# Two 16x16 row substitutions of a gated DeltaNet, put into one set of steps on VectorE

## The chip, the cores and the metric

The kernel runs on one core of one Trainium2 chip. The metric is the device time of one execution in microseconds (us). Engines are TensorE (PE in the rows; its weight loads are PEld), VectorE (DVE), ScalarE (ACT), GpSimd (POOL) and SyncE (SP, which issues the DMAs). Each engine works through its own list of instructions in a fixed order, and semaphores make one engine wait for another.

## What is computed

A backbone of two layers over 256 context tokens and 256 latent tokens. Each layer is a token mixer (three head groups side by side: S5, gated DeltaNet (GDN), Mamba-2) and a feed-forward net (dense in layer 0, eight experts in layer 1). The part at hand is the triangular solve of GDN, once for each direction of the sequence:

```python
kb = k * beta[..., None]
lower = jnp.where(strict, jnp.einsum("bhnid,bhnjd->bhnij", kb, k) * decay, 0.0)
sol = lax.linalg.triangular_solve(jnp.eye(CHUNK, dtype=F32) + lower, rhs,
                                  left_side=True, lower=True, unit_diagonal=True)
```

The second direction is the same on the reversed sequence, so its matrices are triangular the other way.

## The kernel before

The kernel solves by building inverses of the triangular matrices: first those of all 16x16 diagonal blocks, by row substitution, then blocks of 32, 64 and 128 by matrix products. `gdn_prep` makes the 16x16 inverses. The 512 tokens lie as 4 tiles (t) of 128 partitions, with 4 heads (h): a partition is a row of a block, and along the free dimension stand the 16 (t, h) pairs times the 16 columns. So one VectorE instruction works on all 128 blocks (8 along the partitions, 16 along the free dimension) of one direction at once.

For each layer it gathers the diagonal blocks into `c16` (lines 855 to 863), makes for each direction `u` (the block times beta, masked to its triangle, lines 872 and 874) and `x` (set to the identity, line 875), and then takes 15 steps. In each step, for each of the two directions: a stream shuffle on VectorE broadcasts row kk of each block over its 16 partitions (`row`, line 885), a multiply on GpSimd makes `prod` (line 886), and a subtract on VectorE updates the columns of `x` that can be nonzero (line 887). Step number k has n = k+1 columns, so its instructions have 16n elements a partition: 16 to 240. Direction 0 goes down from row 15 with columns kk to 15, direction 1 goes up from row 0 with columns 0 to kk. The two directions don't depend on one another.

What reads the result: `inverses` in `gdn` multiplies `x` into block-diagonal tiles `iv_X` on GpSimd (line 919), and then the products of the levels follow, with `iv_Q` (line 935) and `iv_X` (line 938) on VectorE. The temporary tiles of `gdn_prep` are in a pool that is closed behind it; the pool of `m2_decays` (tiles `dq_r`, `dq_W`, `dq_E`, lines 771, 776, 1065 to 1067) comes to lie on the same memory, so its first tiles wait for the last reader there.

What stands beside it on VectorE: `wL` (line 324), the low half of each weight tile split in two for TensorE (its high half `wH`, line 323, is ScalarE's); the taps of the convolutions `cv_acc` (line 795); in layer 0 the tables of S5 (`cm_a` to `cm_d` and `WV`, lines 430 to 435); the S5 scan (`s5B`, line 607, with its products `s5t` on GpSimd, line 604).

The order on each engine is not written out by hand. A planner fixes it when the program is built: it simulates the engines and picks from what is ready by priority, and the priority is a "band", a number where the smaller goes first. The substitution stands in band 2.0 in layer 0 and 12.62 in layer 1 (`pb`); `wL` in 1.8 and 12.4 (`w`); the qkv convolutions in 2.0 and 12.0, those of Mamba-2 in 3.0 and 13.0 (`xb`); the S5 tables in 1.5 and 2.5; the S5 scan in 3.5 and 12.5; `inverses` in 2.0 to 2.12 and 12.0 to 12.1.

Of the kernel before, what the change touches and what calls it, by code (L numbers as in the profile page):

```python
# [10 lines left out]
F32 = mybir.dt.float32  # L11
# [3 lines left out]
OP = mybir.AluOpType  # L15
# [75 lines left out]
class Net:  # L91
# [741 lines left out]
    def gdn_prep(self, p, tp, kT, qT, bs, sm, t0):  # L833

        nc = self.nc
        sh = [128, 4, 128]
        kw, qw = [], {}
        c32 = tp.tile([128, 4, 4, 32], F32, name="gd_c32")

        def product(f, W, name):  # L840
            ps = self.ps()
            for h in range(4):
                self.mm(ps[:, h * 128:(h + 1) * 128], kT[:, h, sl], f(h), start=True, stop=True, skip_group_check=True)
            m = p.tile(sh, F32, name=name)
            nc.vector.tensor_tensor(m, ps.rearrange("p (h c) -> p h c", h=4), W, op=OP.mult)
            return m

        for t in range(4):
            sl = slice(t * 128, (t + 1) * 128)
            W = tp.tile(sh, F32, name="gd_W")  # L850
            self.decay_quad(tp, sm, t, 16, W, "px", 1)
            kw.append(product(lambda h: kT[:, h, sl], W, f"gd_kw{t}"))
            for q in range(4):
                r = slice(q * 32, q * 32 + 32)
                nc.scalar.activation(c32[r, t], kw[t][r, :, r], AF.Copy)
            if t * 128 >= t0:
                so = slice(t * 128 - t0, (t + 1) * 128 - t0)
                qw[t] = product(lambda h: qT[:, h, so], W, f"gd_qw{t}")
        s16 = [128, 16, 16]
        c16 = tp.tile(s16, F32, name="gd_c16", tag="gd_prod0")  # L860
        cv = c32.rearrange("p t h c -> p (t h) c")
        nc.vector.tensor_scalar(c16, cv[:, :, 0:16], self.half16[:, 0:1], None, op0=OP.mult)
        nc.vector.scalar_tensor_tensor(c16, cv[:, :, 16:32], self.half16[:, 1:2], c16, op0=OP.mult, op1=OP.add)

        def bc(m):
            return m.unsqueeze(1).to_broadcast(s16)

        U, X = [], []
        for d in range(2):
            u = tp.tile(s16, F32, name=f"gd_u{d}")  # L870
            x = p.tile(s16, F32, name=f"gd_x{d}")
            nc.vector.tensor_tensor(u.rearrange("p (t h) c -> p t h c", t=4), c16.rearrange("p (t h) c -> p t h c", t=4),
                                    bs[:, :, d, :].unsqueeze(3).to_broadcast([128, 4, 4, 16]), op=OP.mult)
            nc.vector.tensor_tensor(u, u, bc(self.up16 if d == 0 else self.lo16), op=OP.mult)
            nc.vector.tensor_copy(x, bc(self.id16))
            U.append(u)
            X.append(x)
        for k in range(15):
            for d in range(2):
                kk = 15 - k if d == 0 else k  # L880
                cs = slice(kk, 16) if d == 0 else slice(0, kk + 1)
                n = cs.stop - cs.start
                row = tp.tile(s16, F32, name=f"gd_row{d}")[:, :, :n]
                prod = tp.tile(s16, F32, name=f"gd_prod{d}", tag=f"gd_prod{d}")[:, :, :n]
                nc.vector.stream_shuffle(row, X[d][:, :, cs], [16 * (i // 16) + kk for i in range(32)])
                nc.gpsimd.tensor_tensor(prod, row, U[d][:, :, kk:kk + 1].to_broadcast([128, 16, n]), op=OP.mult)
                nc.vector.tensor_tensor(X[d][:, :, cs], X[d][:, :, cs], prod, op=OP.subtract)
        return kw, qw, X

    def gdn(self, l, p, kT, qT, vD, kD, prep, nrm, bs, ks, qss, sm, szD, yD, t0, b0):  # L890
# [1097 lines left out]
```

## Time and profile before

| | |
|---|---|
| median of 3 runs | 2574.26 us (2572.71 to 2578.19) |
| the profiled execution | 2575.22 us, its span 2573.4 us |
| PE busy | 2384.3 us (93%) |
| DVE busy | 1866.9 us (73%) |
| ACT busy | 1441.4 us (56%) |
| POOL busy | 373.0 us (14%) |

A busy time is summed over the whole span. The page cuts the span into 40 slices of 64 us; the substitution of layer 0 lies in slices 4 and 5 (counted from 1: the fourth and fifth), that of layer 1 in slices 22 and 23. A timeline row gives start, duration, engine, line, operation, tiles, shape and count, and in brackets the idle time of the engine before it with what ended it.

### The profile page before, as it was taken

How to read it: one execution, taken by the hardware profiler on the slowest of the kernel's cores; microseconds unless marked ns; L12 is line 12 of the kernel's file. 1: busy time of each engine (PE TensorE's matmuls, PEld its weight loads, DVE VectorE, ACT ScalarE, POOL GpSimd, SP SyncE). 2: the span in 40 equal slices, each digit the busy share in tenths (PEclk: the TensorE clock that was granted, in tenths of full speed). 3: DMA queues.
4: the chain of work that ended last, by engine and by line, in shares of the span. 5: the costliest groups of instructions: out<-in, count | busy, mean ns of one | idle time of the engine just before them, and what ended most of it. 6: DMA issues, size and time to landing. Idle time of an engine off the chain costs nothing. (4 is left out here: it accounts for less than half of the span.)

```text
span 2573.4 us, 36183 instructions
## 1 busy us (share of the span) xinstructions
PE 2384.3 (93%) x12758; PEld 1864.3 (72%) x12758; DVE 1866.9 (73%) x3011; ACT 1441.4 (56%) x2223; POOL 373.0 (14%) x435
## 2 busy tenths in 40 slices
PE   7999876899999999998988799999999999999997
PEld 4778755556666888886876666587888888888876
DVE  8686998446548765445688954468888888888886
ACT  4676556433234554335766622347777777777765
POOL 0001677312000000000074621100000000000000
PEclk9899988999999999999998899999999999999999
DMA  7343322786635445323543466577999999999993
GB/s 245 114 124 116 119 94 72 238 245 215 233 106 166 146 132 175 103 86 106 163 139 121 152 200 181 171 259 291 346 340 339 356 342 338 353 345 341 353 344 148
DMA packets 222763, 543.87 MB, mean 211 GB/s; under 512 B 26992, under 2 KB 90480, under 8 KB 189552
## 3 DMA queue, kind: packets, MB, share of 16 engines
q1 hardware_dynamic: 222576, 541.50, 61.7%
q8 instruction: 102, 1.67, 0.3%
q14 instruction: 85, 0.70, 0.1%
HBM read 487.87 MB, written 53.54 MB: 210 GB/s over the span
## 5 line engine op out<-in xcount | busy, mean ns | idle before, releaser
L1664 DVE TENSOR_TENSOR mwL<-mwr,mwH 128x2048 fp32r<-128x2048 f32 (+1 forms) x272 | 605.0, 2226 | 95.3 <-PE bank L162 59.8
L1663 ACT ACTIVATE mwH<-mwr 128x2048 fp32r<-128x2048 f32 (+1 forms) x272 | 508.2, 1869 | 202.5 <-PE bank L162 166.4
L323 ACT ACTIVATE wH<-wr 128x512 fp32r<-128x512 f32 (+2 forms) x388 | 232.9, 605 | 400.5 <-PE bank L162 293.7
L324 DVE TENSOR_TENSOR wL<-wr,wH 128x512 fp32r<-128x512 f32 (+2 forms) x388 | 280.9, 726 | 220.2 <-ACT wH L323 199.3
L162 PE MATMUL bank<-mwL,xeH 128*128 128x512 f32 (+1 forms) x768 | 292.7, 381 | 9.3 <-DVE mwL L1664 9.3
L162 PE MATMUL bank<-mwH,xeL 128*128 128x512 f32 (+1 forms) x768 | 288.0, 375 | 0.0
L162 PE MATMUL bank<-mwH,xeH 128*128 128x512 f32 (+1 forms) x768 | 284.6, 376 | 1.7 <-ACT mwH L1663 1.7
L162 PE MATMUL bank<-hH,wH 128*128 128x512 f32 (+2 forms) x656 | 247.5, 385 | 21.8 <-ACT hH L301 8.1
L162 PE MATMUL bank<-hH,wL 128*128 128x512 f32 (+2 forms) x656 | 250.7, 383 | 16.0 <-DVE wL L324 15.9
L162 PE MATMUL bank<-hL,wH 128*128 128x512 f32 (+2 forms) x656 | 248.9, 380 | 1.1 <-DVE hL L302 1.1
L162 PE MATMUL bank<-ada,sc 128*32 128x512 f32 (+1 forms) x576 | 149.7, 503 | 27.0 <-DMA ada<-in_ada_first_dram 13.3
L795 DVE SCALAR_TENSOR_TENSOR cv_acc<-cv_raw,pp,cv_acc 128x512 f32<-128x512 f32 (+1 forms) x192 | 162.8, 861 | 12.1 <-issue 6.1
L162 PEld LDWEIGHTS bank<-mwL,xeH 128*128 128x128 f32 x768 | 144.3, 188 | 37.7 <-DVE mwL L1664 11.7
L162 PEld LDWEIGHTS bank<-mwH,xeH 128*128 128x128 f32 x768 | 144.1, 188 | 31.4 <-ACT mwH L1663 2.5
L162 PEld LDWEIGHTS bank<-mwH,xeL 128*128 128x128 f32 x768 | 144.3, 188 | 26.3
L162 PEld LDWEIGHTS bank<-hH,wH 128*128 128x128 f32 (+1 forms) x656 | 126.5, 194 | 49.6 <-ACT hH L301 10.6
L162 PEld LDWEIGHTS bank<-hH,wL 128*128 128x128 f32 (+1 forms) x656 | 126.7, 193 | 43.9 <-DVE wL L324 20.7
L162 PEld LDWEIGHTS bank<-hL,wH 128*128 128x128 f32 (+1 forms) x656 | 126.8, 193 | 25.8 <-DVE hL L302 2.2
L162 PE MATMUL bank<-mwL,eaH 128*128 128x512 f32 x352 | 139.2, 395 | 0.0
L162 PE MATMUL bank<-fhH,wH 128*128 128x512 f32 x352 | 136.8, 392 | 2.3 <-ACT fhH L301 1.4
L162 PE MATMUL bank<-fhL,wH 128*128 128x512 f32 x352 | 138.8, 394 | 0.0
L162 PE MATMUL bank<-mwH,eaL 128*128 128x512 f32 x352 | 138.6, 394 | 0.0
(440 smaller groups left out, 4715.0 us busy)
## 6 DMA issues: line engine op xcount, KB each, us to landing
mwr<-in_moe_gu_dram SPq DMA_DIRECT2D x176, 1024.0 KB, 5.9
mwr<-in_moe_dn_dram SPq DMA_DIRECT2D x80, 1024.0 KB, 6.1
wr<-in_w_in_dram SPq DMA_DIRECT2D x160, 256.0 KB, 3.0
ada<-in_ada_w_dram SPq DMA_DIRECT2D x128, 256.0 KB, 3.4
wr<-in_w_out_dram SPq DMA_DIRECT2D x64, 256.0 KB, 3.1
wr<-in_ffn_w_gate_dram SPq DMA_DIRECT2D x44, 256.0 KB, 2.7
wr<-in_ffn_w_up_dram SPq DMA_DIRECT2D x44, 256.0 KB, 2.8
ada<-in_ada_first_dram SPq DMA_DIRECT2D x32, 256.0 KB, 5.3
```

The source lines that it names most:

```text
L162: return self.nc.tensor.matmul(*a, **k)
L323: nc.scalar.activation(wH, w, AF.Copy)
L324: nc.vector.tensor_tensor(wL, w, wH.bitcast(F32), op=OP.subtract)
L795: nc.vector.scalar_tensor_tensor(acc, raw[:, :, j:j + 256], w[:, j:j + 1], acc, op0=OP.mult, op1=OP.add)
L1663: nc.scalar.activation(wH, w, AF.Copy)
L1664: nc.vector.tensor_tensor(wL, w, wH.bitcast(F32), op=OP.subtract)
```

## The change

Both directions are put into one tile `X` and one tile `U`, with the direction as an extra dimension. Direction 1 is mirrored: a stream shuffle with a mirrored list of partitions, written through an access pattern of step -1, turns its lower triangle into an upper one, so that both directions take the same steps with the same row and the same columns. A step is then three instructions on VectorE, each with 32n elements: shuffle, multiply (in place in `row`), subtract. GpSimd has no part in it. In the end direction 1 is mirrored back into `x1` and direction 0 copied into `x0`. The temporary tiles need 8 KB a partition where they needed 6 KB. Nothing else is edited.

```diff
-        c16 = tp.tile(s16, F32, name="gd_c16", tag="gd_prod0")
+        c16 = tp.tile(s16, F32, name="gd_c16")
...
-        U, X = [], []
-        for d in range(2):
-            u = tp.tile(s16, F32, name=f"gd_u{d}")
-            x = p.tile(s16, F32, name=f"gd_x{d}")
+        mirror = [16 * (i // 16) + 15 - i % 16 for i in range(32)]
+        U = tp.tile([128, 2, 16, 16], F32, name="gd_u")
+        X = tp.tile([128, 2, 16, 16], F32, name="gd_x")
+        u1 = tp.tile(s16, F32, name="gd_u1")
+        for d in (1, 0):
+            u = u1 if d else U[:, 0]
...
-            nc.vector.tensor_tensor(u, u, bc(self.up16 if d == 0 else self.lo16), op=OP.mult)
-            nc.vector.tensor_copy(x, bc(self.id16))
-            U.append(u)
-            X.append(x)
-        for k in range(15):
-            for d in range(2):
-                kk = 15 - k if d == 0 else k
-                cs = slice(kk, 16) if d == 0 else slice(0, kk + 1)
-                n = cs.stop - cs.start
-                row = tp.tile(s16, F32, name=f"gd_row{d}")[:, :, :n]
-                prod = tp.tile(s16, F32, name=f"gd_prod{d}", tag=f"gd_prod{d}")[:, :, :n]
-                nc.vector.stream_shuffle(row, X[d][:, :, cs], [16 * (i // 16) + kk for i in range(32)])
-                nc.gpsimd.tensor_tensor(prod, row, U[d][:, :, kk:kk + 1].to_broadcast([128, 16, n]), op=OP.mult)
-                nc.vector.tensor_tensor(X[d][:, :, cs], X[d][:, :, cs], prod, op=OP.subtract)
+            nc.vector.tensor_tensor(u, u, bc(self.lo16 if d else self.up16), op=OP.mult)
+        nc.vector.stream_shuffle(U[:, 1, :, ::-1], u1, mirror)
+        nc.vector.tensor_copy(X, self.id16.unsqueeze(1).unsqueeze(1).to_broadcast([128, 2, 16, 16]))
+        for k in range(15, 0, -1):
+            n = 16 - k
+            row = tp.tile([128, 2, 16, 16], F32, name="gd_row")[:, :, :, :n]
+            nc.vector.stream_shuffle(row, X[:, :, :, k:], [16 * (i // 16) + k for i in range(32)])
+            nc.vector.tensor_tensor(row, row, U[:, :, :, k:k + 1].to_broadcast([128, 2, 16, n]), op=OP.mult)
+            nc.vector.tensor_tensor(X[:, :, :, k:], X[:, :, :, k:], row, op=OP.subtract)
+        x1 = p.tile(s16, F32, name="gd_x1")
+        x0 = p.tile(s16, F32, name="gd_x0")
+        nc.vector.stream_shuffle(x1, X[:, 1, :, ::-1], mirror)
+        nc.vector.tensor_copy(x0, X[:, 0])
+        X = [x0, x1]
```

## Rows read from the trace of the kernel before

**Rows 1.** The page: busy tenths of each engine in 40 slices of 64 us.
```profile
PE   7999876899999999998988799999999999999997
DVE  8686998446548765445688954468888888888886
POOL 0001677312000000000074621100000000000000
```

**Rows 2.** Stretches: us, busy time (instructions) per engine, granted clock, DMA share, GB/s.
```profile
253.00:280.00 27.00, 27.00 (x129) 22.38 (x127) 23.97 (x95) 16.37 (x24) 13.22 (x23) 1.00 0.54 157
280.00:450.00 170.00, 120.48 (x658) 97.97 (x656) 160.66 (x204) 97.19 (x199) 122.27 (x116) 0.88 0.26 85
...
1380.00:1400.00 20.00, 12.12 (x37) 8.58 (x35) 11.86 (x45) 19.75 (x29) 6.77 (x16) 0.83 0.44 158
...
1400.00:1480.00 80.00, 67.06 (x339) 52.72 (x340) 79.42 (x137) 52.28 (x119) 49.58 (x58) 0.89 0.49 155
1480.00:1640.00 160.00, 158.56 (x1023) 104.05 (x1021) 76.51 (x151) 46.44 (x121) 28.87 (x26) 1.00 0.64 189
```

**Rows 3.** Waits from 250 to 480 us: total, times, longest.
```profile
PE bank L162 <- DVE iv_Q L935: 22.3, 7, 7.3
```

**Rows 4.** Groups of instructions by line: count, busy us, mean ns, idle before.
```profile
L886 POOL TENSOR_TENSOR gd_prod<-gd_row,gd_u 128x16 f32<-128x16 f32 (+14 forms) x60 | 38.1, 645 | 57.5 <-DVE gd_row L885 40.4 <-DVE gd_u L874 16.1
...
L887 DVE TENSOR_TENSOR gd_x<-gd_x,gd_prod 128x16 f32<-128x16 f32 (+14 forms) x60 | 20.8, 362 | 2.5 <-POOL gd_prod L886 1.9
L885 DVE STREAM_SHUFFLE gd_row<-gd_x 128x16 f32<-128x16 f32 (+14 forms) x60 | 18.0, 328 | 0.0
```

**Rows 5.** Timeline of VectorE in layer 0: substitution, S5 tables, `wL`, convolution.
```profile
253.58 0.42 DVE L430 TENSOR_TENSOR cm_a<-WV,mr 128x256 f32<-128x256 f32 x1
253.91 0.42 DVE L431 TENSOR_TENSOR cm_c<-WV,mi 128x256 f32<-128x256 f32 x1
...
256.74 0.22 DVE L885 STREAM_SHUFFLE gd_row<-gd_x 128x32 f32<-128x32 f32 x1
...
269.17 0.28 DVE L887 TENSOR_TENSOR gd_x<-gd_x,gd_prod 128x112 f32<-128x112 f32 x1
...
269.49 0.28 DVE L885 STREAM_SHUFFLE gd_row<-gd_x 128x128 f32<-128x128 f32 x1
...
279.73 0.68 DVE L324 TENSOR_TENSOR wL<-wr,wH 128x512 fp32r<-128x512 f32 x1
...
289.50 1.13 DVE L795 SCALAR_TENSOR_TENSOR cv_acc<-cv_raw,pp,cv_acc 128x512 f32<-128x512 f32 x1
...
290.56 0.43 DVE L885 STREAM_SHUFFLE gd_row<-gd_x 128x240 f32<-128x240 f32 x1
290.89 0.39 DVE L887 TENSOR_TENSOR gd_x<-gd_x,gd_prod 128x240 f32<-128x240 f32 x1
...
292.23 1.29 DVE L887 TENSOR_TENSOR gd_x<-gd_x,gd_prod 128x240 f32<-128x240 f32 x1
```

**Rows 6.** Timeline of GpSimd just after the substitution of layer 0.
```profile
291.71 2.76 POOL L771 TENSOR_SCALAR_AFFINE_SELECT dq_r<-la 128x1024 fp32r<-128x1024 f32 x2
```

**Rows 7.** Timeline of VectorE in layer 1, columns as in rows 5.
```profile
1387.88 0.69 DVE L324 TENSOR_TENSOR wL<-wr,wH 128x512 fp32r<-128x512 f32 x1 [4.05 <-ACT wH L323]
...
1410.88 0.33 DVE L887 TENSOR_TENSOR gd_x<-gd_x,gd_prod 128x176 f32<-128x176 f32 x1
1411.14 0.74 DVE L795 SCALAR_TENSOR_TENSOR cv_acc<-cv_raw,pp,cv_acc 128x512 f32<-128x512 f32 x1
1411.81 0.37 DVE L885 STREAM_SHUFFLE gd_row<-gd_x 128x192 f32<-128x192 f32 x1
...
1432.48 0.39 DVE L887 TENSOR_TENSOR gd_x<-gd_x,gd_prod 128x240 f32<-128x240 f32 x1
```

**Rows 8.** Stretches with the GpSimd products alone (line 886), columns as in rows 2.
```profile
253.00:293.00 40.00, 18.16 (x30) 1.00 0.44 132
1361.00:1433.00 72.00, 19.91 (x30) 0.91 0.39 132
```

## The prediction

> **What bounds the kernel now.** I read the busy tenths of the page first. PE is at nine tenths nearly everywhere, with two dips, in slices 5 to 7 and around 21 to 23; in both VectorE (DVE) stands at eight or nine tenths, and GpSimd (POOL) does nearly all of its work there [rows 1]. The two substitutions lie at the front of these dips. Then I cut the dips into stretches. In layer 0 PE is full up to 280 us, and VectorE has 3 us of slack in those 27 us; from 280 to 450 VectorE is busy 160.7 of 170 us and PE 120.5 [rows 2]. In layer 1 VectorE is full from 1400 to 1480 (79.4 of 80 us, PE 67.1), and from 1480 PE is full again [rows 2]. The list of waits says the same: PE's largest wait for VectorE in the first dip is 22.3 us for `iv_Q` [rows 3]. So time that VectorE saves after 280 and after 1400 us comes off the end, and time that it saves or spends elsewhere does not.
>
> **Second, what the substitution costs.** The groups by line: 60 products on POOL, 38.1 us, and before them POOL idles 40.4 us for `row`; 60 subtracts on VectorE, 20.8 us; 60 shuffles, 18.0 us [rows 4]. VectorE waits for a product only 1.9 us in all, because the planner lays `wL`, the tables or `cv_acc` into the gap, and because the two directions cover one another. So the hop to POOL and back is long, but it is hardly VectorE that pays for it.
>
> **The change, part by part.** All sums are per layer; there are two.
>
> *Lengths.* A two-input operation takes 0.28 us at 112 elements, 0.39 at 240, 0.42 at 256 and 0.68 at 512 [rows 5]: about 0.15 us and 1.04 ns an element. A shuffle takes 0.22 at 32, 0.28 at 128, 0.37 at 192 and 0.43 at 240 [rows 5, 7]: about 0.15 us and 0.073 us for each 64 elements begun.
>
> *Removed from VectorE.* 30 shuffles and 30 subtracts of 16n elements, n from 1 to 15, twice: 9.7 + 8.5 = 18.2 us without disturbance.
>
> *Added to VectorE.* 15 shuffles of 32n elements: 15 x 0.15 + 64 x 0.073 = 6.9 us. 15 products and 15 subtracts, 3840 elements each in sum: 30 x 0.15 + 7680 x 1.04 ns = 12.5 us. Together 19.4 us: moving the product over is almost paid for by halving the count. A shuffle of 480 elements and one with a reversed output are not in the trace; the line through the rows gives the first 0.73 us, and the reversed one I take like a plain one of 256 elements, 0.44 us, between 0.22 (the shortest shuffle) and twice that value. The rest of the preparation adds two such shuffles and one copy and joins two copies to one: about 1.0 us, between 0.6 and 2.
>
> *How they overlap.* These lengths are not what VectorE is held for. Two operations that don't need each other start 0.33 us apart where each lasts 0.42, so each costs its length less 0.09; one that needs the one in front starts at its end plus 0.04 (269.17 + 0.28 to 269.49) [rows 5]. Before, two directions alternate: 18.2 - 60 x 0.09 = 12.8 us. After, every one of the 45 needs the one in front. If the planner lays something between, they cost 19.4 - 45 x 0.09 = 15.3 us; if nothing, 19.4 + 45 x 0.04 = 21.2 us. Both happen today: at 1410.88 to 1411.81 a `cv_acc` stands between subtract and shuffle [rows 7], at 269.17 nothing does [rows 5]. I take a third of the way in layer 0, and nearly the filled end in layer 1, where `cv_acc` and `wL` abound; both ends stay in the range.
>
> *Removed with the products: the disturbance.* Beside a GpSimd operation VectorE's two-input ones get longer: a subtract of 240 elements 1.29 us where its twin takes 0.39, a `cv_acc` 1.13 where it takes 0.74 [rows 5, 7]. Summing, for each VectorE row that overlaps a product, what it is longer than the shortest of its shape, I get 4.4 us in layer 0 and 6.3 in layer 1; the products themselves grow from 18.2 us to 19.9 in layer 1 [rows 8]. The `cv_acc` at 289.50 is one of 19 such rows in layer 0, with 0.40 us. The subtract at 292.23 is none of them: it runs beside `dq_r`, which stays [rows 6]. By the Trainium skill (SBUF — State Buffer, Who interferes with whom) a VectorE instruction with two SBUF inputs and a GpSimd one that reads SBUF exclude one another, and the second waits until the first has ended; by that rule each of the 60 products could cost its whole length, 38 us in sum rather than some 10. The rows show the lengthening, but mostly far less than a product's length, so the sum goes by the rows.
>
> *Layer 0.* The substitution starts at 254 us. Until 280 VectorE also has some 18 table operations of 0.33 and 9 `wL` of 0.60 to do, and 1.4 us of waiting: 13 us. With 16.3 to 22.2 us of its own (15.3 to 21.2 and 1.0) the substitution ends at 283 to 289, where it now ends at 293.5 [rows 5]. What lies before 280 is covered by PE's full 27 us [rows 2]; were PE not full there, 1 to 4 us more would show. After 280 there are now 15 of its operations, some 4.6 us, with 2.4 us of the disturbance: 7 us. After the change 3 to 9 us remain. A gain of 4 to a loss of 2; I take a gain of 2.5.
>
> *Layer 1.* VectorE is held now for 12.8 + 6.3 + 1.0 (waits for POOL) = 20.1 us, and then for 16.3 to 22.2: a gain of 3.8 to a loss of 2.1. Of VectorE's 8 us of slack at 1380 to 1400 [rows 2] 4 are one `wL` that waits for ScalarE [rows 7]; in-order chain steps behind it wait too, now as then. I take a gain of 4.
>
> *What comes earlier.* `dq_r` starts on POOL right behind the last product [rows 6], and `iv_X` waits for the last subtract, at 1432.9 in layer 1 [rows 7]. In layer 1 a late step takes about 5 us now (four VectorE operations, each with `wL` or `cv_acc` between) and would take 3 to 3.5, so `x` is ready 10 to 20 us sooner. That moves work forward into a stretch where VectorE is already full, so I count nothing for it; at its best it fills PE's 13 us of idle time at 1400 to 1480. The planner also fixes all orders anew, and no row shows what that does: one badly placed operation costs up to the 7.3 us of PE's longest wait for `iv_Q` [rows 3], one better placed gains as much. I take nothing, and keep both ends.
>
> **Sum.** 2.5 + 4 = 6.5 us. The profiled execution took 2575.2 us, 1.0 above the median of the runs shown; so 2568.7 in its terms, 2567.7, say 2568, as a median. A measurement of this kernel tells about 0.2% (5 us) from no change.
>
> **The rivals.** *No change* (2572 to 2577 us): the 45 steps stand half alone, VectorE's time is the same, and the gain in disturbance is spent on gaps. For it: 18.2 against 19.4 us is a draw, and POOL was no bound. Against it: the planner's filling.
>
> *More than forecast* (2552 to 2560): the earlier `x` counts, inverses and decays spread into PE's idle time of both dips, and 15 to 20 us go. For it: 22.3 us of waiting for `iv_Q`. Against it: VectorE is full there.
>
> *Slower* (2580 to 2588): the chain on VectorE becomes the bound of the dips. Each of 45 steps alone costs 21.2 + 1.0 where 12.8 + 1.0 were paid, 8.4 us a layer, and the 30 two-input operations are now themselves exposed to POOL's remaining work (`s5t`, `dq_r`), at 0.9 us for each one hit, as at 292.23 [rows 5]; seven hits in layer 1 are 6 us. Against it stand the 4.4 and 6.3 us of disturbance removed; it decides from about two thirds of the steps alone. In sum 6 to 12 us. The Trainium skill (Perfetto Trace Analysis, Optimizing Scalar/DVE Operations) says that handing some work to GpSimd may make sense where VectorE is saturated, though the two share a read port: taken alone, that speaks for the kernel before, and it is this rival.
>
> That the change doesn't do what it says (products left on POOL) is excluded by the diff.
>
> **How the numbers follow.** Forecast, 2562 to 2571: 40%. More: 10%. No change: 25%. Slower: 25%. Faster by over 0.2% means under 2569: all of "more" and 36 of the forecast's 40, 46%. Within 0.2%: 4 + 25 = 29%. Slower: 25%. The range leaves out a tenth at either end: 2555 to 2585. Cases of both signs hold most of the chance, so the forecast's own range, 2562 to 2571, stands beside it.
>
> **What would show it.** POOL's busy sum falls by about 38 us to 335; VectorE's stays within 5 us of its 1867. The new shuffle and product lines show 30 operations each with means near 0.46 and 0.42 us. `cv_acc` and `wL` in 277 to 293 and 1400 to 1433 return to 0.74 and 0.68. The last `x` is written near 286 and 1415. If the shuffles with 480 elements or the reversed one take over 1 us, if gaps on VectorE at the chain's lines sum to more than 5 us a layer, or if new waits of PE appear outside the two dips, the prediction is wrong.

## The result and the profile after

The kernel after takes 2593.01 us (median of 5 runs, 2589.45 to 2598.38), the kernel before 2573.90 (5 runs, 2566.67 to 2578.19): a ratio of 1.0082, 95% interval 1.0061 to 1.0102. It is slower by 19 us. The forecast was 2568, with 2555 to 2585 as its range.

The profiled execution after took 2593.01 us with a span of 2591.3. Its busy tenths, as in [rows 1], show that GpSimd has lost most of its work in the two dips, and that TensorE (PE) has not gained by it:

```profile
PE   7999876899988999998987799998999999999997
DVE  8676997446549675445688854467888888888886
POOL 0011557412000000000071431100000000000000
```

GpSimd is busy 332.2 us where 335 were forecast, VectorE (DVE) 1860.9 where "within 5 us of its 1867" was forecast: 6.0 less. The new lines, with count, busy us and mean ns (line numbers are those of the kernel after: product, shuffle, subtract):

```profile
L884 DVE TENSOR_TENSOR gd_row<-gd_row,gd_u 128x32 f32<-128x32 f32 (+14 forms) x30 | 15.9, 529 | 0.3
L883 DVE STREAM_SHUFFLE gd_row<-gd_x 128x32 f32<-128x32 f32 (+14 forms) x30 | 14.9, 496 | 0.0
L885 DVE TENSOR_TENSOR gd_x<-gd_x,gd_row 128x32 f32<-128x32 f32 (+14 forms) x30 | 14.6, 488 | 0.3
```

The three lines hold VectorE for 45.4 us in the two layers, where 38.8 were forecast; most of the excess is operations that got longer beside GpSimd (last section). VectorE idles next to nothing in front of them. The stretches say where the time is lost (columns as in [rows 2], same stretches):

```profile
280.00:450.00 170.00, 119.43 (x656) 98.48 (x655) 155.79 (x201) 92.74 (x197) 113.53 (x106) 0.88 0.26 85
...
1400.00:1480.00 80.00, 61.56 (x296) 48.18 (x296) 68.35 (x117) 43.29 (x91) 21.15 (x33) 0.86 0.42 134
1480.00:1640.00 160.00, 153.81 (x957) 100.10 (x956) 80.61 (x150) 48.27 (x133) 41.00 (x35) 0.98 0.59 173
```

In layer 0's dip VectorE has become freer by 4.9 us (160.66 to 155.79), and PE does about as much as before. In layer 1's, 1400 to 1480, VectorE falls from 79.42 to 68.35 us and PE from 67.06 to 61.56 [rows 2]: the engine that was full now stands idle for 11.6 of 80 us, and TensorE does less. In that stretch VectorE now waits 5.6 us for ScalarE in front of `cv_acc`, and 5.1 for products of TensorE in front of `iv_Q` and `iv_X`. An engine that is relieved and a bound engine that idles more suggest that both wait for a chain. (In this execution layer 1 begins 4.3 us later than before, so the stretches are not quite the same work.) The granted clock of the whole span is no lower, 0.970 after and 0.968 before.

The chain itself, on VectorE's timeline in layer 1, columns start, length, line, operands; one whole step and the start of the next:

```profile
1418.47 0.59 DVE L883 STREAM_SHUFFLE gd_row<-gd_x 128x352 f32<-128x352 f32 x1
1418.95 0.67 DVE L324 TENSOR_TENSOR wL<-wr,wH 128x512 fp32r<-128x512 f32 x1
1419.54 0.74 DVE L795 SCALAR_TENSOR_TENSOR cv_acc<-cv_raw,pp,cv_acc 128x512 f32<-128x512 f32 x1
1420.20 0.51 DVE L884 TENSOR_TENSOR gd_row<-gd_row,gd_u 128x352 f32<-128x352 f32 x1
1420.64 0.74 DVE L795 SCALAR_TENSOR_TENSOR cv_acc<-cv_raw,pp,cv_acc 128x512 f32<-128x512 f32 x1
1421.30 0.68 DVE L324 TENSOR_TENSOR wL<-wr,wH 128x512 fp32r<-128x512 f32 x1
1421.90 0.74 DVE L795 SCALAR_TENSOR_TENSOR cv_acc<-cv_raw,pp,cv_acc 128x512 f32<-128x512 f32 x1
1422.56 0.51 DVE L885 TENSOR_TENSOR gd_x<-gd_x,gd_row 128x352 f32<-128x352 f32 x1
1423.00 0.74 DVE L795 SCALAR_TENSOR_TENSOR cv_acc<-cv_raw,pp,cv_acc 128x512 f32<-128x512 f32 x1
1423.66 0.67 DVE L324 TENSOR_TENSOR wL<-wr,wH 128x512 fp32r<-128x512 f32 x1
1424.27 0.73 DVE L795 SCALAR_TENSOR_TENSOR cv_acc<-cv_raw,pp,cv_acc 128x512 f32<-128x512 f32 x1
1424.94 0.59 DVE L883 STREAM_SHUFFLE gd_row<-gd_x 128x384 f32<-128x384 f32 x1
...
1452.67 0.28 DVE L889 COPY gd_x<-gd_x 128x256 f32<-128x256 f32 x1
```

Everything is as short as forecast (shuffle 0.59, product 0.51, `wL` 0.67, `cv_acc` 0.74, no lengthening), and yet one step takes 6.47 us (1418.47 to 1424.94), of which its own three instructions hold VectorE for 1.4, from start to start. Eight others lie between. From the first product to the last subtract layer 1 has 76 such others in 77.1 us; before there were 61 in 70.9 us. `x` was ready at 1432.9 [rows 7] and is now at 1453.0. In layer 0 the chain grew from 40.1 to 49.3 us.

The steps are not the whole way to `x`. The last masked `u` is ready at the same place in the layer as before (194.7 us after its first matmul, before 194.4). Before, GpSimd's first product started on it at once; its row:

```profile
1361.97 0.95 POOL L886 TENSOR_TENSOR gd_prod<-gd_row,gd_u 128x16 f32<-128x16 f32 x2 [0.36 <-DVE gd_u L874]
```

After, the mirror of `u` comes first, and at the end the mirror and the copy of `x`, each in VectorE's queue behind other work:

```profile
1369.56 0.44 DVE L878 STREAM_SHUFFLE gd_u<-gd_u 128x256 f32<-128x256 f32 x1
...
1371.85 1.29 DVE L884 TENSOR_TENSOR gd_row<-gd_row,gd_u 128x32 f32<-128x32 f32 x1
...
1448.30 0.64 DVE L885 TENSOR_TENSOR gd_x<-gd_x,gd_row 128x480 f32<-128x480 f32 x1
1451.93 0.48 DVE L795 SCALAR_TENSOR_TENSOR cv_acc<-cv_raw,pp,cv_acc 128x256 f32<-128x256 f32 x1 [3.00 <-ACT cv_acc L793]
...
1452.34 0.44 DVE L888 STREAM_SHUFFLE gd_x<-gd_x 128x256 f32<-128x256 f32 x1
```

Counted from the layer's first matmul, `x` is 15.8 us later than before: the first product starts 5.6 us later, the steps take 6.2 us more, and 4.0 us pass behind the last subtract, 3.0 of them with VectorE idle for a `cv_acc` that stands in front of the mirror.

### The profile page after: what moved, and what is told of

It reads as the page before. It is cut to its first block, busy times and chain, and to the rows that moved or that the text cites. A ratio compares the mean times of both kernels' runs of the same rounds, so it can differ in the third digit from the quotient of the medians.

```text
span 2591.3 us, 36003 instructions
## 1 busy us (share of the span) xinstructions
PE 2383.6 (92%) x12758; PEld 1866.4 (72%) x12758; DVE 1860.9 (72%) x2959; ACT 1429.6 (55%) x2213; POOL 332.2 (13%) x375
## 5 line engine op out<-in xcount | busy, mean ns | idle before, releaser
L324 DVE TENSOR_TENSOR wL<-wr,wH 128x512 fp32r<-128x512 f32 (+2 forms) x388 | 274.6, 711 | 230.5 <-ACT wH L323 213.4
L162 PE MATMUL bank<-hH,wH 128*128 128x512 f32 (+2 forms) x656 | 247.4, 385 | 26.1 <-ACT cv_acc L793 10.8
L162 PEld LDWEIGHTS bank<-mwL,xeH 128*128 128x128 f32 x768 | 144.3, 188 | 37.6 <-DVE mwL L1667 11.6
L795 DVE SCALAR_TENSOR_TENSOR cv_acc<-cv_raw,pp,cv_acc 128x512 f32<-128x512 f32 (+1 forms) x192 | 154.2, 818 | 17.3 <-ACT cv_acc L791 10.1
```

The lines of the kernel that those rows point to most:

```text
L162: return self.nc.tensor.matmul(*a, **k)
L324: nc.vector.tensor_tensor(wL, w, wH.bitcast(F32), op=OP.subtract)
L795: nc.vector.scalar_tensor_tensor(acc, raw[:, :, j:j + 256], w[:, j:j + 1], acc, op0=OP.mult, op1=OP.add)
```

## The experiments

All of them keep the rest of the kernel. Layer 0 and layer 1 call the same preparation, so the first two runs put the new one into one layer only:

```
+ prep = (self.gdn_prep_new if l == 0 else self.gdn_prep)(pg, p, kT, qT, sc[1], sm, t0)
```

> The change in layer 0 alone; layer 1 keeps the kernel before. Theory Q (visits): a step is now three instructions that need one another, each queued on VectorE behind weight splits and convolution taps, where a direction's step had two such visits and a hop to GpSimd; what hurts is that x comes later in layer 1, where the inverses and the output projection follow straight behind. By Q layer 0 is the small part: 2576 to 2581 us, x of layer 0 near 305 us as in the changed kernel, and the layer-0 loss shows only behind 640 us. Rival P (planning): the loss is an accident of the orders fixed anew, and layer 0 is as likely to hold it: anything from 2570 to 2595, layer 1 shifted too. Rival D (VectorE's work in the two dips): half of the loss here, 2583.

Measured: 2585.55 us (2582.27 to 2587.8), ratio 1.0050 (1.0032 to 1.0068). Above theory Q's range and near D's number; the later runs on layer 0 look for the cause.

> The change in layer 1 alone; layer 0 keeps the kernel before. Q: 2585 to 2590 us, some 15 of the 19 us; the last write of x at about 1447 us where it was 1432.9, the first iv_X product and the first output projection later by the same 14 to 16 us. P: no fixed tie between the end of x and the output projection. D: half of the loss, 2583, with VectorE busier by 5 us or more between 1360 and 1480.

Measured: 2590.97 us (2586.91 to 2598.79), ratio 1.0070 (1.0047 to 1.0093). As Q said, `x` comes late, at 1452.5 us. Each layer loses by itself, 12 and 17 us; together they lose 19, not 29.

Then the two halves of the change, each alone. The mirrored, joined steps with the product left on GpSimd (`nc.vector` to `nc.gpsimd` in the product):

> The mirrored, joined steps as in the changed kernel, but the product stays on GpSimd: 15 steps of two VectorE instructions and one GpSimd instruction, in both layers. Q: two visits a step as before, and half as many instructions, so x of layer 1 is ready no later than before (1415 to 1435 us) and the time is 2565 to 2578. D: VectorE has a third less to do than in the changed kernel, so the kernel gains on before, 2560 to 2570. P: the orders are new here too, so 2580 to 2595 is as likely.

Measured: 2591.85 us (2589.47 to 2594.04), ratio 1.0073 (1.0051 to 1.0095). The forecast of Q fails: with half the instructions of the kernel before, the steps of layer 1 take 71.4 us, no less than its 70.9. A likely reason is that each product costs the way to GpSimd and back, which the second direction no longer covers. `x` is ready 7.6 us later, counted from the layer's first matmul, and 7.1 of them are the mirrors and the copy: 4.1 in front of the first product, 3.0 behind the last subtract.

The two separate directions kept, the product moved to VectorE (`nc.gpsimd` to `nc.vector` in the kernel before):

> The kernel before with only the engine of the product changed: two directions side by side, 90 instructions a layer on VectorE, three visits a step for each direction. Q: x of layer 1 late by 10 us or more (after 1443), and 2583 to 2595 us. D: VectorE gets 8.5 us of products a layer less the disturbance of 4 to 6, so 2576 to 2582. P: the orders differ little from those of before, so 2572 to 2577.

Measured: 2600.35 us (2597.02 to 2605.13), ratio 1.0105 (1.0079 to 1.0131). That is above every theory's range. The steps of layer 1 take 78.3 us, 7.4 more than before, and `x` is 10.8 us late, as Q said. By the medians the products' move alone costs more than the whole change, and the joining wins a part of that back.

**Taking the other operations out of the chain.** If they are what makes it long, then holding each step's three instructions together in layer 1 should bring the loss back. The edit, abridged, wraps each step and orders its instructions by a semaphore of its own:

```
+ with self.tc.tile_critical():
      shuffle.then_inc(csem, 1); nc.vector.wait_ge(csem, 2 * (15 - k) + 1)
      product.then_inc(csem, 1); nc.vector.wait_ge(csem, 2 * (15 - k) + 2)
      subtract
```

> The change in layer 1 alone, with the three instructions of each of the 15 steps held together: nothing can be laid between shuffle, product and subtract, only between steps. By the order 12 other operations remain between the first step and the last, where 77 ran. Theory F (what costs is the time until x is ready, and that is set by the other operations that VectorE does between dependent instructions): the chain lasts 25 to 35 us instead of 77.1, the inverses begin some 40 us earlier, the 17 us that the change costs in layer 1 go, and some of them come back as a gain: 2564 (2556 to 2574). Theory V (what costs is VectorE's own time in the mirrored steps, or the planner's other order of layer 1, and not the chain's length): the chain gets short too, but the time stays at 2585 to 2596, since the same work has to be done by VectorE in the same stretch.

Measured: 2609.73 us (2604.04 to 2611.26), ratio 1.0143 (1.0124 to 1.0163). The whole chain as one block:

> The change in layer 1 alone, with all 45 instructions held together as one block, nothing else between. Theory F: the chain lasts 20 to 23 us; x is ready as early as in the run with whole steps or 5 to 10 us earlier; but VectorE does no `wL` and no `cv_acc` meanwhile, so TensorE waits some 5 to 10 us for weights: 2566 (2556 to 2578). Theory V: 2585 to 2600.

Measured: 2608.75 us (2605.2 to 2614.2), ratio 1.0139 (1.0114 to 1.0163). Both theories fall. The chains did get short (51.4 and 21.8 us from their first shuffle, `x` ready some 13 and 42 us before the kernel before, counted from the layer's first matmul), and the time got worse by another 18 us. The waits of TensorE in the run with one block, 1360 to 1480 us (total, times, longest):

```profile
PE bank L162 <- DVE wL L324: 28.9, 2, 22.9
```

and its stretch:

```profile
1360.00:1400.00 40.00, 13.72 (x51) 10.42 (x50) 37.65 (x80) 6.92 (x16) 16.50 (x14) 0.69 0.15 46
```

So the "others" in the chain are not waste: the `wL` among them are what TensorE lives on. While VectorE does 21.8 us of substitution at a stretch, TensorE has no weights and stands for 22.9. With whole steps it waits 14.6 us for `wL` and then 24.7 once for `iv_X`; holding has a price of its own too: VectorE stood idle some 21 us in front of the held steps, 8.1 of it once.

**Making the chain shorter without taking VectorE away from `wL`.** This leaves out steps, in layer 1 of the run with the change there only (`range(15, 0, -1)` to `range(15, 3, -1)`, and to `range(15, 8, -1)`), and in layer 1 of the kernel before (`range(15)` to `range(11)`):

> The change in layer 1 alone, and there the last 3 of the 15 steps are left out, so that the two directions' results lack the last three columns' contribution. By the order 51 other operations remain inside the chain instead of 77, and x is ready some 20 us sooner, about where the kernel before has it. Theory X (TensorE runs out of projections at about 1435 us and then waits for the inverses, which wait for x; so each us by which x comes after that point costs one): the 17 us of the change in layer 1 go: 2576 (2570 to 2582). Theory V (VectorE's own time in the steps is the price): three steps of some 1.4 us are saved, 2587 (2583 to 2592). Theory R (the planner's other order, whatever the chain's length): 2587 to 2596.

Measured: 2569.93 us (2566.4 to 2575.78, 10 runs), ratio 0.9997 (0.9986 to 1.0009). The whole loss of layer 1 is gone, 21 us by leaving out 3 steps that hold VectorE for some 5 (19.3 to 14.1). That is in favour of theory X (its range ended at 2570) and against V and R.

> The change in layer 1 alone, and there the last 8 of the 15 steps are left out; 19 other operations remain inside the chain, and x is ready some 45 to 55 us sooner than with all steps, well before TensorE has run out of projections. Theory X: the gain ends there, since before the projections' end nothing waits for x; with some 8 us less of VectorE's work: 2570 (2562 to 2577), hardly under the run without 3 steps. Rival S (what the runs with held steps showed, 2609, was that an early x harms by itself, because the inverses' work is put ahead of the projections' on VectorE): 2590 or more.

Measured: 2581.12 us (2579.83 to 2583.58), ratio 1.0043 (1.0028 to 1.0058). Between the two: a far earlier `x` is not worth more, it costs 11 us against the run without 3 steps.

> The kernel before, and in layer 1 the last 4 of the 15 steps of both directions are left out, so x is ready some 20 us sooner than in the kernel before, at about 1412 us: what the prediction counted on. Theory X: x is ready then before TensorE runs out of projections, so at most the 8.5 us in which TensorE idles at 1440 to 1480 can come back: 2569 (2564 to 2574). The prediction's own view (an earlier x is worth nothing, VectorE's own time is worth all): the 16 left-out operations of about 0.41 us are 6.5 us: 2567 (2564 to 2570). Rival S: slower than before, 2578 or more.

Measured: 2576.51 us (2571.42 to 2581.37, 10 runs), ratio 1.0019 (1.0007 to 1.0031). With less work and `x` some 20 us sooner, the kernel before gains nothing: the time lies above what X and the prediction's view allow, and below what S asks for.

All these runs on one scale: us from layer 1's first matmul (its norm) to `x` ready, to the last matmul of the input projections, and to the first of the experts that follow the layer; then where layer 1 begins, in us from the start of the span, and the run's median. From the experts on all of them take the same, 822 to 825 us.

| run | `x` ready | projections end | experts begin | layer 1 begins | time |
|---|---|---|---|---|---|
| before | 265.1 | 264.5 | 582.8 | 1167.8 | 2574 |
| layer 1 without 3 steps | 259.2 | 265.0 | 582.7 | 1167.9 | 2569.9 |
| before without 4 steps | 244.5 | 287.1 | 583.6 | 1162.6 | 2576.5 |
| layer 1 without 8 steps | 227.5 | 298.1 | 587.2 | 1166.6 | 2581.1 |
| product on GpSimd | 272.7 | 264.8 | 594.2 | 1171.4 | 2591.9 |
| two directions on VectorE | 275.9 | 267.9 | 592.7 | 1181.2 | 2600.4 |
| after | 280.9 | 263.9 | 596.3 | 1172.1 | 2593.0 |
| change in layer 1 alone | 282.1 | 264.8 | 599.8 | 1170.4 | 2591.0 |
| steps held whole | 251.8 | 333.8 | 614.2 | 1165.3 | 2609.7 |
| chain as one block | 223.5 | 324.4 | 616.8 | 1166.0 | 2608.8 |

The kernel before has `x` and the end of the projections within 1 us of each other. An `x` that comes later delays the experts by about as much (after: 15.8 us late, 13.5 lost; layer 1 alone: 17.0 and 17.0; two directions on VectorE: 10.8 and 9.9; product on GpSimd: 7.6 and 11.4), while the projections end at 264 to 268 as before. An `x` that comes earlier by 20.6 or 37.6 us gains nothing: the inverses then go first, the projections end 22.6 or 33.6 us later, and the experts begin 0.8 or 4.4 us later. The planner orders layer 1 anew in each run, so the time of `x` and the order that it leads to are not told apart here; that the loss follows `x` is what the table shows.

What TensorE waits for in the gap, 1435 to 1465 us, in the kernel after:

```profile
PE bank L1108 <- DMA m_in<-mD: 6.5, 1, 6.5
PE bank L1106 <- DVE m_S L1132: 4.0, 1, 4.0
PE bank L1106 <- DMA m_in<-mD: 3.0, 1, 3.0
```

and how much it does there, in the kernel after, then without the 3 steps in layer 1:

```profile
1435.00:1465.00 30.00, 13.55 (x52) 8.78 (x51) 26.90 (x43) 12.92 (x34) 12.59 (x16) 0.70 0.52 158
```

```profile
1435.00:1465.00 30.00, 20.48 (x105) 15.89 (x106) 29.11 (x41) 20.63 (x44) 20.94 (x23) 0.89 0.56 178
```

The names mislead here. TensorE waits for Mamba-2's inputs from DRAM, and only 0.7 us go to an `iv_X`, which needs `x`: behind the projections the order has Mamba-2's states first, and the inverses begin at 1455.4, behind `x`. Without the 3 steps, with `x` in time, the waits for `m_in` are gone (the longest are then 6.1 us for `iv_Z` and 3.3 for `iv_Q`). The list of waits shows what stood in the queue, not what should have stood there.

**Layer 0.** Until about 640 us the kernel after is ahead: `iv_Q` ends at 569.2 us instead of 578.9. Then Mamba-2's last group, `m_in`, ends at 717.5 instead of 668.4, since the planner has put a run of 134 matmuls of the out-projection in front of it on TensorE. First that group alone was moved, by its band (`m2o=3.9` to `1.05`), with the change in layer 0 only, and in the kernel before:

> The change in layer 0 alone, and Mamba-2's output products there given the band 1.05 instead of 3.9, so that the planner lays the last four groups ahead of the out-projection on TensorE instead of behind 138 of its matmuls. Theory O (layer 0's 12 us are lost where the planner laid those last groups behind the out-projection; the longer chain itself costs nothing there): `m_in` ends at 675 or earlier where it ended at 719, `yo` by 705 instead of 737, and the time is 2571 (2566 to 2577). Theory D (the longer chain delays everything after it, by its 11.5 us): 2581 to 2588, as with the change in layer 0 alone (2585.6).

Measured: 2586.45 us (2579.69 to 2588.36, 7 runs), ratio 1.0041 (1.0025 to 1.0058). `m_in` ends at 654 and `yo` at 697, as theory O wanted, and the time stays: S5's output had now been pushed behind it, and the out-projection began at 673.6 instead of 655.2.

> Control: the kernel before with the same band, 1.05 instead of 3.9, for Mamba-2's output products in layer 0; the last groups stand ahead of the out-projection there already. Theory O: within 4 us of the kernel before (2570 to 2578). If it gains as much as the run with the change in layer 0 gains by it (10 us or more), the band is a gain by itself and says nothing of the change.

Measured: 2579.96 us (2572.23 to 2585.68, 10 runs), ratio 1.0023 (1.0010 to 1.0036). A band that changes no work costs 6 us in the kernel before.

> The change in layer 0 alone, and there the last 4 of the 15 steps are left out, so that the chain is about as short as in the kernel before (27 other operations inside instead of 41). The order on TensorE at the end of layer 0 stays as with all steps: 138 matmuls of the out-projection ahead of Mamba-2's last group. Theory O (layer 0's loss is the order at its end, not the chain): `m_in` still ends at 708 or later and the time is 2580 to 2587. Theory D (the longer chain delays what follows): `m_in` ends at 675 or earlier, 2570 to 2577.

Measured: 2573.06 us (2566.28 to 2580.58, 10 runs), ratio 1.0010 (0.9994 to 1.0025), with `m_in` only at 701.6, between the two theories' places, and the 134 matmuls still in front of it: the time is D's, the order is O's. A shorter chain makes good the bad order.

So the next run kept the chain long and restored the order of both (`m2o=1.05`, `sb=1.04`):

> The change in layer 0 alone, with two bands in layer 0 moved, Mamba-2's output products to 1.05 (from 3.9) and S5's output to 1.04 (from 3.5), so that TensorE's order at the end of layer 0 is nearly that of the kernel before: S5's output, then Mamba-2's last products, then the out-projection from the same place in the queue. The run with Mamba-2 moved alone had pushed S5's output to the end instead. Theory O (what the change loses in layer 0 is the order at the hand-over to the out-projection, while the longer chain itself leaves layer 0 some 6 us ahead until 640 us): out-projection from 650 to 662, layer 1 begins at 1160 to 1170, 2570 (2563 to 2577). Theory D (the longer chain costs by itself, wherever the order lets it show): out-projection from 668 or later, 2582 to 2589.

Measured: 2572.87 us (2568.91 to 2579.8, 12 runs), ratio 1.0000 (0.9989 to 1.0011). The 12 us are gone with all 15 steps in place; the out-projection begins at 650.1 us, as theory O wanted. The control:

> Control: the kernel before with the same two bands. Its order at the end of layer 0 hardly moves. Expected 2576 (2571 to 2582): no gain by the bands alone. If it falls below 2570, the bands are a gain of their own, and the run with the change has to be read against it.

Measured: 2576.18 us (2571.6 to 2578.81, 12 runs), ratio 1.0007 (0.9998 to 1.0016): the bands are no gain of their own. The stretch 780 to 900 us shows where the order's price falls, with the change in layer 0 only, then with the order kept:

```profile
780.00:900.00 120.00, 110.90 (x534) 85.32 (x534) 98.32 (x334) 53.15 (x98) 0.00 (x0) 0.99 0.36 116
```

```profile
780.00:900.00 120.00, 119.04 (x585) 90.17 (x584) 90.68 (x312) 54.18 (x94) 0.00 (x0) 1.00 0.49 154
```

TensorE loses 8.1 us after the layer, at the start of the feed-forward part: the modulation's matmuls that fill its first waits end at 787 us in the first run and at 805 in the second. The stretch is not the whole account: from 640 to 780 the first run has 3.6 us more of TensorE's work. By where layer 1 begins in these two traces, 1175.7 and 1166.6 us, the order is worth some 9 us. Last, the whole change with these bands:

> The whole change, with the same two bands in layer 0 (1.05 and 1.04). Layer 0's loss goes by the bands, so what is left is layer 1's. If the two layers' losses stand apart, layer 1 alone is left with the 17 us that it costs in the run with the change there only: 2590 (2585 to 2595). If they were parts of a sum of 19, as the medians of the whole change would have it (12 of it layer 0's), 2581 (2577 to 2585).

Measured: 2592.86 us (2583.03 to 2594.8, 6 runs), ratio 1.0063 (1.0042 to 1.0083). Layer 1's loss stays whole; in the trace `x` is ready 282.3 us into the layer and the experts begin at 597.8, as in the other runs with the change there. The trace is of one of the two runs at 2583 us; the other four lie at 2592 to 2595. In it layer 1 begins at 1161.6 us, so here layer 0 loses nothing. The trace of the whole change without these bands has layer 1 beginning at 1172.1, while seven traces with layer 0 as before have it between 1162.6 and 1170.4: little of the 12 us was there to be won back. Why the median does not move is open.

No run beat the kernel before by more than its interval.

## Why the prediction was wrong

**Its lengths were right.** They came out: a shuffle of 480 elements at 0.71 to 0.75 (forecast 0.73), the reversed one at 0.44, products and subtracts of 480 at 0.64 to 0.65 where no other engine interferes. The chain's instructions sum to 21.6 us in layer 1, of which two hit by GpSimd are 2.0 too long; 19.4 were forecast. GpSimd's sum and the vanished lengthening of `cv_acc` and `wL` from 1400 us on are as said. VectorE's sum fell by 6.0, just outside the 5 it allowed; the means of the new lines are 496 and 529 ns where 460 and 420 were forecast. The 4 us taken as layer 1's gain lie above the upper end of its own sum, 3.8.

**The step that failed first is the bound:** "time that VectorE saves after 280 and after 1400 us comes off the end". VectorE was busy 4.9 us less from 280 to 450 and 11 less from 1400 to 1480, and the kernel got slower; with 4 steps left out of layer 1 the kernel before gained nothing either (2576.5 us, where that view gave 2567). In layer 1 the time followed `x`, so what failed with it is "What comes earlier". It said that a late step in layer 1 takes about 5 us and would take 3 to 3.5, so that `x` would be ready 10 to 20 us sooner. It takes 6.5, and `x` is 15.8 us later. The estimate took one other operation between each two instructions, because rows 7 show one between a subtract and a shuffle; there were 1.8 on average (76 in 43 gaps), and two or three in the late steps. Before, two independent directions shared VectorE, so that the operations between served both, and the products ran on GpSimd meanwhile. After, three dependent visits in a row each wait for their own. This makes 6.2 of the 15.8 us. The other 9.6 are the mirrors and the copy, which the prediction put at about 1.0 us: that is their time on VectorE, and they stand in the way to `x` with their waits in the queue. The count that mattered was visits in sequence, not time on VectorE.

**Its price was wrong too.** The prediction counted nothing for the time of `x`, in either direction. For an earlier `x` that is right, by the runs without steps; for a later one it is wrong, by the table: the projections end where `x` was ready. The signs were there: [rows 2] show TensorE at 67.06 of 80 us from 1400 to 1480 and full from 1480, and its largest wait in that stretch before was for `iv_Q`, 5.2 us (in layer 0 it was 22.3 [rows 3]), so inverses are what it then lacked.

**The slower rival** had the right engine and place ("the chain on VectorE becomes the bound of the dips") and the wrong price: it added up VectorE's time for steps that stand alone, 6 to 12 us. In layer 1 the steps that stand alone were the cheap ones; those with cover made the chain long.

**The new order** was put at 7.3 us at most, gain or loss, and at nothing in the sum. When the change stands in layer 0 alone, 12 us are lost. Restoring the order brings them back, and so does a shorter chain in the bad order, so the loss needs both. With the order restored the forecast for layer 0 itself (a gain of 2.5) is not contradicted: 2572.9 against 2576.2 for its control, within their intervals. The prediction named new waits outside the dips as a sign of being wrong; they came at 780 to 900 us, 480 us behind the edit.

That a product beside `s5t` would cost about 0.9 us extra, as in the slower rival, came true in layer 0 (1.1, below).

## What to carry to other kernels

A chain of dependent instructions in an engine's fixed queue costs its visits times what a planner lays between them. Moving a link from a slow engine to a busy one saves the hop and adds a visit: here the steps got longer by it, from 70.9 to 78.3 us with two directions and from 71.4 to 77.1 with the joined ones. Joining two independent chains halved the instructions and left the steps about as long, and what reshapes the data in front and behind, 1 us of work, was 7 to 11 us of way. Before trading, look up when the chain's result is first lacking: here it was ready within 1 us of the moment at which the other work ran out, so later cost about one for one and earlier paid nothing. And before blaming the others in the chain, ask who lives on them: taken out, they cost TensorE more than the chain had.

## What the hardware showed

Where VectorE and GpSimd both had a row of two-input operations, the lengths fit taking turns. In layer 0 the last steps ran against the S5 multiplications, which the planner had moved up from 297 to 288 us. GpSimd, four operations in one row, 1.70 us each:

```profile
288.28 6.80 POOL L604 TENSOR_TENSOR s5t<-s5B,s5l 128x512 f32<-128x512 f32 x4 [4.34 <-ACT s5B L574]
```

VectorE beside it, and one product and one subtract of 480 elements after it, the second of them begun ahead of GpSimd's next operation (303.09):

```profile
290.51 1.72 DVE L884 TENSOR_TENSOR gd_row<-gd_row,gd_u 128x448 f32<-128x448 f32 x1
292.14 1.77 DVE L795 SCALAR_TENSOR_TENSOR cv_acc<-cv_raw,pp,cv_acc 128x512 f32<-128x512 f32 x1
293.84 1.72 DVE L885 TENSOR_TENSOR gd_x<-gd_x,gd_row 128x448 f32<-128x448 f32 x1
...
298.99 1.75 DVE L884 TENSOR_TENSOR gd_row<-gd_row,gd_u 128x480 f32<-128x480 f32 x1
...
302.93 0.65 DVE L885 TENSOR_TENSOR gd_x<-gd_x,gd_row 128x480 f32<-128x480 f32 x1
```

Each VectorE operation takes as long as one of GpSimd's, 1.72 to 1.77 us whatever its size, 1.0 to 1.1 more than alone. The Trainium skill (SBUF — State Buffer, Who interferes with whom) says that such operations contend for a shared port pair, which is an exclusive lock; these rows agree, where the rows of the kernel before mostly showed far less than a product's length.

The shuffle's length goes in steps of 128 elements in the new shape (two by 16 by n): 0.30 us at 96 and 128 elements, 0.43 at 160 to 256, 0.59 at 288 to 384, 0.71 to 0.75 at 416 to 480. At 192 elements it takes 0.43 where the old shape took 0.37 [rows 7]. In sum this changes little, 7.1 us for 14 of them in layer 1.
